# First five pairs of the up projection: low parts of the weight operands and one sum made by accumulating DMAs instead of VectorE

## The chip, the cores and the metric

The kernel runs on one core of a Trainium2 chip. The metric is the device time of one execution in microseconds (us). The kernel before takes 2647.08 us (median of 3 runs, 2645.2 to 2648.05). The core has a matrix engine (TensorE, in the profile PE, with its weight loads as PEld), VectorE (DVE), ScalarE (ACT), GpSimd (POOL) and SyncE (SP). Each takes its instructions in order from its own queue. Transfers (DMAs) are issued by SP, ACT and POOL and run on 16 shared DMA engines.

## The reference

Two layers of an encoder trunk over 1040 positions (16 learned meta tokens and 1024 inputs) with width 1024. Each layer is an attention part followed by a gated feed-forward part. Only the second matters here:

```
def conv_ffn(x, w_up, conv_w, conv_b, w_down):
    h = x @ w_up
    L = h.shape[1]
    hp = jnp.pad(h, ((0, 0), (CONV_W - 1, 0), (0, 0)))
    hc = conv_b
    for j in range(CONV_W):
        hc = hc + hp[:, j:j + L] * conv_w[j]
    u, g = jnp.split(hc, 2, axis=-1)
    return (jax.nn.silu(g) * u) @ w_down

...
        h = h + jnp.concatenate([o_gla, o_fox], axis=-1) @ w_out[i]
        h = h + conv_ffn(rms_norm(h, ffn_norm[i]), w_up[i], conv_w[i], conv_b[i], w_down[i])
```

`w_up` has 2 x 2816 columns: 22 blocks of 128 columns for u and 22 for g. All data is float32.

## The kernel before

**The product scheme.** Every float32 matrix product is made from two parts of each operand: `hi`, the operand rounded to the reduced format that the matrix engine multiplies (fp32r), and `lo`, the operand minus `hi`. Three matmuls (hi x hi, lo x hi, hi x lo; `mm3`, L216 to L218) replace one.

The up projection of a layer (`ffn_up`) takes the 22 pairs (u block j, g block j) one after the other. For each pair the weights form a 2 x 2 block matrix: rows are u and g, columns are the two halves of the 1024 inputs. A11 and A12 are the halves of u, A21 and A22 those of g. The positions are also cut in two halves of 520 (516 in the second layer). A scheme with seven block products instead of eight, numbered p = 1 to 7, is used. Its weight operands are A11 (p = 1), A12 (2), A12 - S2 (3), A22 (4), S1 = A21 + A22 (5), S2 = S1 - A11 (6) and A11 - A21 (7). The other operands, X1 to X7, are made once per layer from the normalised positions. Each product (j, p) is 4 x 2 x 3 = 24 matmuls of 128 x 260 (258) columns.

**The order of products** is written out by hand in `seq`; PE follows it exactly. For the first three pairs it is (0,1) (0,2) (1,1) (1,2) (2,1) (2,2), then (0,6) (1,6) (0,7) (1,7) (0,4) (1,4) (0,5) (1,5) (0,3) (1,3), then the rest of pair 2. From j = 3 on it is (j,2) (j,6) (j,5) (j,7) (j+1,1) (j,4) (j,3). The instructions of the other engines are ordered by a scheduler when the kernel is built, so each engine's queue is fixed before it runs.

**Weight operands.** `ensure(i)` calls `up_operand` for products up to four ahead (`AHEAD = 4`). At the first use of a pair, SP loads the four raw blocks of 128 x 512 (256 KB each). A11 and A12 go to tag `raw` (4 buffers), A21 and A22 to tag `raw2`, whose pool has 7 buffers. `combine` makes S1 and S2 (two more `raw2` buffers) and rewrites A21 and A12 in place, all on VectorE (L997). For (2,1) and (2,2) the blocks of pair 2 are loaded once more, early, each into a `raw2` buffer (L983). `up_split` then makes `hi` with a copy on ACT (L1013) and `lo` with a subtraction on VectorE (L1014). `hi` and `lo` have 3 buffers for even and 3 for odd products. A buffer is reused when the last instruction that reads it has ended.

**X operands.** X1 and X2 are made during the output projection that precedes (`wout`). `second_half` (before product 1) scales the norm of the second half. `make_t23` (before product 2) makes X6 and X7: L1132, L1133 and the splits of `put` (ACT L1037, VectorE L1038). `make_n4` and `make_t1` make X4 and X5 with subtractions on POOL (L1144, L1152), `make_b22` X3. `wout` also stores each block of h to memory from POOL (L1096) and adds squares on POOL (L1102).

**Results.** A product fills a pair of PSUM banks. `place` gives the bank: products p = 2 of the pairs 0, 1 and 2 all use the bank pair `p2`. `evacuate` copies p = 1, 4, 6, 7 out on ACT (L1181) and adds p = 2, 3 and the g sum on VectorE (L1180). So (1,2) waits for VectorE's addition after (0,2), and (2,2) for the one after (1,2). When a pair is complete, `conv` (ACT L1169, VectorE L1173) and the gate follow, and POOL stores the block (`actd`, L1203).

Of the kernel before, what the change touches and what calls it, by code (L numbers as in the profile page):

```python
# [10 lines left out]
F32 = mybir.dt.float32  # L11
# [3 lines left out]
ALU = mybir.AluOpType  # L15
# [33 lines left out]
HALVES, HALVES_LAST = (0, 520, 520), (8, 524, 516)  # L49
AHEAD = 4  # L50
NSPLIT = 4


class Slots:
# [78 lines left out]
class Kern:  # L133
# [731 lines left out]
    def attention(self, lyr, nm, hsrc, chunks, feed):  # L865
        tc, nc, s = self.tc, self.nc, self.slots
        with tc.tile_pool(name=f"aps{lyr}", bufs=2, space=PSUM, reuse_waits="tile") as pp2, \
# [50 lines left out]
            with tc.tile_pool(name=f"att{lyr}", bufs=2, reuse_waits="tile") as ap, \  # L918
# [5 lines left out]
                def plan(p):  # L924
# [11 lines left out]
                    elif p == 4:  # L936
# [10 lines left out]
                        def split(j):  # L947
                            c0, n = CH[j]
                            for k in KORD:
                                self.split(mix[k][0][:, c0:c0 + n], mix[k][1][:, c0:c0 + n], land[k][:, c0:c0 + n])  # L950
                            for m in range(NSPLIT):
                                nc.gpsimd.dma_start(hT[m][:, c0:c0 + n], hsrc[m][:, c0:c0 + n])
                        split(2)
                        for m in range(NSPLIT):
                            def ev(ps, c0, n, m=m):
                                h = hT[m][:, c0:c0 + n]
                                nc.vector.tensor_tensor(out=h, in0=ps, in1=h, op=ALU.add)
# [3 lines left out]
                self.fox(lyr, ap, pp, qs, plan, lambda: box["mix"][KD - 1])  # L961
            for m in range(NSPLIT, KD):
                nc.sync.dma_start(box["hT"][m][:, chunks[0][0]:T], hsrc[m][:, chunks[0][0]:T])
# [15 lines left out]
    def up_operand(self, lyr, j, p, fw, raws, odd):  # L979
        nc = self.nc  # L980
        if j == 2 and p in (1, 2):
            src = fw.tile([128, 4, 128], F32, tag="raw2", name="raw2")
            nc.sync.dma_start(src[:], self.wm[lyr, M_UP + 4][:, 4 * p - 4:4 * p, :])  # L983
            return self.up_split(src, fw, odd)
        if j not in raws:
            u, g = self.wm[lyr, M_UP + 2 * j], self.wm[lyr, M_UP + 2 * j + 1]
            q = raws[j] = {}
            for name, src, k0, own in (("A11", u, 0, True), ("A21", g, 0, False), ("A22", g, 4, False), ("A12", u, 4, True)):
                q[name] = self.wp.tile([128, 4, 128], F32, tag="raw", name="raw", bufs=4) if own else \
                    fw.tile([128, 4, 128], F32, tag="raw2", name="raw2")  # L990
                nc.sync.dma_start(q[name][:], src[:, k0:k0 + 4, :])
        q = raws[j]

        def combine(out, a, b, op):
            if out not in q:
                q[out] = fw.tile([128, 4, 128], F32, tag="raw2", name="raw2")
            nc.vector.tensor_tensor(out=q[out][:], in0=q[a][:], in1=q[b][:], op=op)  # L997
        if p == 6:
            combine("S1", "A21", "A22", ALU.add)
            combine("S2", "S1", "A11", ALU.subtract)  # L1000
        elif p == 7:
            combine("A21", "A11", "A21", ALU.subtract)
        elif p == 3:
            combine("A12", "A12", "S2", ALU.subtract)
        src = q[{1: "A11", 2: "A12", 3: "A12", 4: "A22", 5: "S1", 6: "S2", 7: "A21"}[p]]
        return self.up_split(src, fw, odd)

    def up_split(self, src, fw, odd):
        nc = self.nc
        pool, x = (fw, "2") if odd else (self.wp, "")  # L1010
        hi = pool.tile([128, 4, 128], F32R, tag="hi" + x, name="hi", bufs=3)
        lo = pool.tile([128, 4, 128], F32R, tag="lo" + x, name="lo", bufs=3)
        nc.scalar.copy(hi[:], src[:])  # L1013
        nc.vector.tensor_tensor(out=lo[:], in0=src[:], in1=hi[:].bitcast(F32), op=ALU.subtract)  # L1014
        return [(hi[:, k, :], lo[:, k, :]) for k in range(4)]

    def ffn_up(self, lyr, mix, hT, pp, fw, halves, o0, during_last):
# [65 lines left out]
        def wout(i, h):  # L1083
            m = orders[h][i]
            k0 = KD - 1 if m < NSPLIT else 0

            def f(w):
# [15 lines left out]
                if h == 0:  # L1103
                    return
                if m < NSPLIT:
                    nc.scalar.mul(half(gt, m % 2), x, gain(m))
# [327 lines left out]
```

## Time and profile before

| | |
|---|---|
| median of 3 runs | 2647.08 us (2645.2 to 2648.05) |
| the profiled execution | 2645.09 us |
| its span, first to last instruction | 2643.3 us |
| busy: PE, PEld | 2523.9, 2407.2 us |
| busy: DVE, ACT, POOL | 1759.9, 1240.1, 457.9 us |
| mean granted clock of TensorE | 0.987 |
| matmuls named `up` by line | 3 x 2464 = 7392 |

Times in the profile are microseconds from the start of the span. A row of the timeline gives start, duration, engine, line, operation, output tile <- input tiles, shape, and in brackets how long the engine sat idle before it and what ended that. In the first layer the up projection starts at 612.4 us; its steady part takes about 20.1 us for a pair. Busy time is an average over stages; what an edit is worth is read from the stage that it touches.

### The profile page before, as it was taken

To read this page: it belongs to the slowest core of one execution; us is meant where nothing else is said; L and a number is where in the kernel's file an instruction comes from. 1 tells how busy PE (TensorE), PEld (TensorE's weight loads), DVE (VectorE), ACT (ScalarE), POOL (GpSimd) and SP (SyncE) were. 2 spreads that over 40 slices of the span, in tenths; PEclk is the share of its full clock that TensorE was granted. 3 is DMA by queue.
4 is the path that set the end of the run, shared out by engine and by line. 5 is a ranking of instruction groups with operands and counts; after the bars stand their busy time and mean duration, and the time that the engine had idled before them with its cause. 6 is when DMAs were issued, how large, how long until landed. Compare 5 with 4: busy or idle time off the path is not lost.

```text
span 2643.3 us, 46336 instructions
## 1 busy us (share of the span) xinstructions
PE 2523.9 (95%) x18102; PEld 2407.2 (91%) x18102; DVE 1759.9 (67%) x3484; ACT 1240.1 (47%) x2677; POOL 457.9 (17%) x596
## 2 busy tenths in 40 slices
PE   8999999897999999999999999998989999999997
PEld 7988898897999999999999888887889999998886
DVE  7655676759877777643665666666698767776335
ACT  6345665645544445421343565665455444453112
POOL 4033333333000000000201333332320000000002
PEclk9999999998999999999999999999999999999999
DMA  3222124341222222632312222142512222245222
GB/s 125 65 83 70 47 83 124 106 131 58 97 81 76 85 77 92 217 94 58 103 56 65 75 72 74 56 138 91 158 51 85 83 81 77 83 139 189 65 55 77
DMA packets 114476, 240.72 MB, mean 91 GB/s; under 512 B 14432, under 2 KB 36192, under 8 KB 114256
## 3 DMA queue, kind: packets, MB, share of 16 engines
q1 hardware_dynamic: 96000, 182.27, 22.7%
q0 software_dynamic: 16384, 53.18, 5.5%
q8 instruction: 142, 2.33, 0.4%
q10 hardware_dynamic: 1872, 2.31, 0.2%
q14 instruction: 78, 0.64, 0.1%
HBM read 174.01 MB, written 50.91 MB: 85 GB/s over the span
## 4 chain that ended last, share of the span: by engine, by line
PE 77%; DVE 13%; ACT 4%; issue 3%; DMA 2%; POOL 2%; DVEq 0%; SPq 0%; POOLq 0%; ACTq 0%
PE mm L216 12%; PE mm L217 12%; PE mm L218 12%; PE up L216 10%; PE up L217 10%; PE up L218 10%; PE av L706 2%; PE tr L688 2%; DVE S L655 1%; DVE x L1038 1%; PE wo L217 1%; PE wo L216 1%; PE wo L218 1%; DVE PT L331 1%; ACT P L667 1%
## 5 line engine op out<-in xcount | busy, mean ns | idle before, releaser
L216 PE MATMUL up<-x,hi 128*128 128x260 f32 (+1 forms) x2464 | 701.3, 285 | 22.7 <-DVE hu L1180 20.3
L217 PE MATMUL up<-x,lo 128*128 128x260 f32 (+1 forms) x2464 | 699.2, 284 | 0.0
L218 PE MATMUL up<-x,hi 128*128 128x260 f32 (+1 forms) x2464 | 698.5, 283 | 0.0
L216 PEld LDWEIGHTS up<-x,hi 128*128 128x128 f32 x2464 | 467.5, 190 | 24.4 <-DVE hu L1180 20.7
L217 PEld LDWEIGHTS up<-x,lo 128*128 128x128 f32 x2464 | 467.9, 190 | 0.1
L218 PEld LDWEIGHTS up<-x,hi 128*128 128x128 f32 x2464 | 467.8, 190 | 0.0
L216 PE MATMUL mm<-xh,hi 128*128 128x348 f32 (+4 forms) x1056 | 365.1, 346 | 0.0
L218 PE MATMUL mm<-xl,hi 128*128 128x348 f32 (+4 forms) x1056 | 340.9, 323 | 0.0
L217 PE MATMUL mm<-xh,lo 128*128 128x348 f32 (+4 forms) x1056 | 340.8, 323 | 0.0
L1014 DVE TENSOR_TENSOR lo<-raw,hi 128x512 fp32r<-128x512 f32 x308 | 212.9, 694 | 146.2 <-ACT hi L1013 146.2
L183 ACT CAST hi<-raw 128x512 fp32r<-128x512 f32 (+1 forms) x264 | 142.3, 543 | 329.8 <-PE mm L218 240.0
L217 PE MATMUL mm<-ah,lo 128*128 128x400 f32 (+1 forms) x760 | 266.4, 351 | 0.2 <-DVE lo L185 0.2
L218 PE MATMUL mm<-al,hi 128*128 128x400 f32 (+1 forms) x760 | 265.9, 350 | 0.0
L216 PE MATMUL mm<-ah,hi 128*128 128x400 f32 (+1 forms) x760 | 265.8, 350 | 0.0
L185 DVE TENSOR_TENSOR lo<-raw,hi 128x512 fp32r<-128x512 f32 (+1 forms) x196 | 120.7, 620 | 181.1 <-ACT hi L183 177.5
L1013 ACT CAST hi<-raw 128x512 fp32r<-128x512 f32 x308 | 190.3, 620 | 107.6 <-PE up L218 92.7
L216 PEld LDWEIGHTS mm<-xh,hi 128*128 128x128 f32 x1056 | 201.0, 190 | 6.0 <-issue 5.3
L217 PEld LDWEIGHTS mm<-xh,lo 128*128 128x128 f32 x1056 | 200.9, 190 | 0.4 <-issue 0.3
L218 PEld LDWEIGHTS mm<-xl,hi 128*128 128x128 f32 x1056 | 199.9, 189 | 0.4 <-issue 0.3
L1203 POOL DMA_DIRECT2D actd<-cv x44 | 23.4, 533 | 830.0 <-DVE cv L1202 830.0
L667 ACT ACTIVATE P<-S,m 116x460 f32<-116x460 f32 (+2 forms) x224 | 124.8, 561 | 76.9 <-DVE m L655 72.6
L331 DVE TENSOR_TENSOR PT<-tr,PT 116x464 fp32r<-116x464 f32 (+3 forms) x240 | 122.1, 516 | 55.8 <-ACT PT L330 54.1
(248 smaller groups left out, 5269.0 us busy)
## 6 DMA issues: line engine op xcount, KB each, us to landing
raw<-in_wm_dram SPq DMA_DIRECT2D x328, 256.0 KB, 2.6
raw<-in_wd_dram SPq DMA_DIRECT2D x64, 256.0 KB, 2.6
actd<-cv POOLq DMA_DIRECT2D x22, 520.0 KB, 2.9
st<-actd SPq DMA_DIRECT2D x22, 520.0 KB, 4.9
actd<-cv POOLq DMA_DIRECT2D x22, 512.0 KB, 3.0
st<-actd SPq DMA_DIRECT2D x22, 512.0 KB, 4.8
cb<-cd SPq DMA_DIRECT2D x16, 520.0 KB, 4.2
kA<-kA SPq DMA_DIRECT2D x24, 260.0 KB, 3.8
```

Of the source, the lines that this page charges most:

```text
L183: nc.scalar.copy(hi[:, :n, :], raw[:, :n, :])
L185: eng.tensor_tensor(out=lo[:, :n, :], in0=raw[:, :n, :], in1=hi[:, :n, :].bitcast(F32), op=ALU.subtract)
L216: nc.tensor.matmul(ps, wh, xh[:, c0:c0 + n], start=first, stop=False, skip_group_check=more)
L217: nc.tensor.matmul(ps, wl, xh[:, c0:c0 + n], start=False, stop=False, skip_group_check=more)
L218: nc.tensor.matmul(ps, wh, xl[:, c0:c0 + n], start=False, stop=last, skip_group_check=more)
L331: nc.vector.tensor_tensor(out=lo, in0=src, in1=hi.bitcast(F32), op=ALU.subtract)
L655: nc.vector.tensor_tensor_reduce(out=S[:rows, :n], in0=S[:rows, :n], in1=cb[:rows, c0:k1], scale=1.0, scalar=(BIG if ci == 0 else m[:rows, ...
L667: nc.scalar.activation(P[:rows, :n], S[:rows, :n], AF.Exp, scale=-1.0, bias=m[:rows, nch - 1:nch], accum_out=(den if nch == 1 else d3[:row ...
L688: nc.tensor.transpose(tr[:w, j, :rows], P[:rows, o:o + w], id_)
L706: nc.tensor.matmul(av[:, a:width], w.rearrange("p a b -> p (a b)"), x, start=(t == 0 and i == 0), stop=(t == last and i == 1))
L1013: nc.scalar.copy(hi[:], src[:])
L1014: nc.vector.tensor_tensor(out=lo[:], in0=src[:], in1=hi[:].bitcast(F32), op=ALU.subtract)
```

## The change

For pairs j = 0 to 4 (`N_DMA_LO = 5`) of both layers:

- `lo` is no longer a subtraction on VectorE. ACT writes -hi into the `lo` tile, and a DMA issued by POOL adds the raw block to it in place (`accum_op=ALU.add`).
- S1 is no longer an addition on VectorE. SP loads the first half of g into a `raw2` buffer once more, and a DMA issued by POOL adds the second half to it from memory. This buffer is taken at the first use of the pair, not at p = 6.

The early blocks of (2,1) and (2,2) are treated the same way. S2, A11 - A21 and A12 - S2 stay on VectorE. All other pairs are as before.

```
+N_DMA_LO = 5
...
         if j == 2 and p in (1, 2):
             src = fw.tile([128, 4, 128], F32, tag="raw2", name="raw2")
             nc.sync.dma_start(src[:], self.wm[lyr, M_UP + 4][:, 4 * p - 4:4 * p, :])
-            return self.up_split(src, fw, odd)
+            return self.up_split(src, fw, odd, True)
...
                 nc.sync.dma_start(q[name][:], src[:, k0:k0 + 4, :])
+            if j < N_DMA_LO:
+                q["S1"] = fw.tile([128, 4, 128], F32, tag="raw2", name="raw2")
+                nc.sync.dma_start(q["S1"][:], g[:, 0:4, :])
+                nc.gpsimd.dma_start(q["S1"][:], g[:, 4:8, :], accum_op=ALU.add)
...
         if p == 6:
-            combine("S1", "A21", "A22", ALU.add)
+            if "S1" not in q:
+                combine("S1", "A21", "A22", ALU.add)
             combine("S2", "S1", "A11", ALU.subtract)
...
-        return self.up_split(src, fw, odd)
+        return self.up_split(src, fw, odd, j < N_DMA_LO)
...
-    def up_split(self, src, fw, odd):
+    def up_split(self, src, fw, odd, by_dma):
...
         nc.scalar.copy(hi[:], src[:])
-        nc.vector.tensor_tensor(out=lo[:], in0=src[:], in1=hi[:].bitcast(F32), op=ALU.subtract)
+        if by_dma:
+            nc.scalar.mul(lo[:], hi[:].bitcast(F32), -1.0)
+            nc.gpsimd.dma_start(lo[:].bitcast(F32), src[:], accum_op=ALU.add)
+        else:
+            nc.vector.tensor_tensor(out=lo[:], in0=src[:], in1=hi[:].bitcast(F32), op=ALU.subtract)
```

Counted in the built programs, the queues change by -80 instructions on VectorE, +70 on ACT, +80 DMAs on POOL and +10 loads on SP, over both layers. PE's order is the same, and outside the first pairs so are the other queues.

## The prediction

> **What bounds the kernel now.** I read the page first, then PE's waits, then the timelines around the one wait that matters, then a table of stretches.
>
> ```profile
> span 2643.3 us, 46336 instructions
> PE 2523.9 (95%) x18102; PEld 2407.2 (91%) x18102; DVE 1759.9 (67%) x3484; ACT 1240.1 (47%) x2677; POOL 457.9 (17%) x596
> PE up L216 <- DVE hu L1180: 20.3, 2, 10.2
> PE up L216 <- ACT hu L1181: 2.1, 2, 1.1
> core 0: us, PE busy (x) PEld busy (x) DVE busy (x) ACT busy (x) POOL busy (x), PEclk, DMA share, GB/s
> 628.30:638.40 10.10, 0.00 (x0) 0.00 (x0) 8.98 (x12) 6.09 (x11) 4.36 (x3) 0.61 0.00 1
> 638.40:654.00 15.60, 14.50 (x97) 14.29 (x98) 14.77 (x20) 6.03 (x11) 5.13 (x3) 0.82 0.17 51
> 700.00:720.10 20.10, 20.10 (x170) 20.10 (x169) 14.79 (x20) 9.71 (x14) 0.53 (x1) 1.00 0.22 80
> ```
>
> PE is busy 95% of the span, and in the steady part of the up projection (last row, about one pair) all of the time, with VectorE at 14.79 of 20.10 us. VectorE work saved there buys nothing. The only large PE wait in the up projection is 20.3 us in two pieces, one per layer, for a VectorE addition into `hu`. That is where this change can pay.
>
> ```profile
> 619.65 0.70 DVE L273 SCALAR_TENSOR_TENSOR nt<-nt 128x520 f32<-128x520 f32 x1
> 620.27 0.70 DVE L1180 TENSOR_TENSOR hu<-up,hu 128x520 f32<-128x520 f32 x1
> 620.87 0.70 DVE L274 TENSOR_TENSOR nt<-nt 128x520 f32<-128x520 f32 x1
> 621.48 0.69 DVE L1014 TENSOR_TENSOR lo<-raw,hi 128x512 fp32r<-128x512 f32 x1
> 629.42 0.70 DVE L1038 TENSOR_TENSOR x<-h,x 128x520 fp32r<-128x520 f32 x1 [2.38 <-ACT x L1037]
> 637.71 0.69 DVE L1180 TENSOR_TENSOR hu<-up,hu 128x520 f32<-128x520 f32 x1
> 638.46 0.59 PE L216 MATMUL up<-x,hi 128*128 128x260 f32 x1 [10.25 <-DVE hu L1180]
> 653.80 0.40 PE L216 MATMUL up<-x,hi 128*128 128x260 f32 x1 [1.05 <-ACT hu L1181]
> ```
>
> Product (2,2) needs bank `p2`, which (1,2) filled. The addition that empties it starts at 637.71 and ends at 638.40, because it stands in VectorE's queue behind `make_t23` (X6, X7) and the operand work. Queued instructions follow each other every 0.61 us (619.65, 620.27, 620.87, 621.48).
>
> **What goes and what comes.**
>
> ```profile
> L1014 DVE TENSOR_TENSOR lo<-raw,hi 128x512 fp32r<-128x512 f32 x308 | 212.9, 694 | 146.2 <-ACT hi L1013 146.2
> L997 DVE TENSOR_TENSOR raw<-raw,raw 128x512 f32<-128x512 f32 x176 | 116.0, 698 | 0.2
> L1013 ACT CAST hi<-raw 128x512 fp32r<-128x512 f32 x308 | 190.3, 620 | 107.6 <-PE up L218 92.7 <-DVE raw L997 7.7 <-PE wo L218 7.2
> L1096 POOL DMA_DIRECT2D hm<-h x16: 547/549/562, 557.7 to 613.8; - x16
> L991 SPq DMA_DIRECT2D raw<-in_wm_dram x176: 327/328/433, 540.8 to 2321.7; - x176
> ```
>
> VectorE loses 70 subtractions x 0.694 = 48.6 us and 10 additions x 0.698 = 7.0 us. ACT gains 70 scalings; the nearest row is its cast, 0.620, so 43 us. POOL gains 80 DMA issues x 0.55 = 44 us, SP 10 loads x 0.33 = 3 us. In a steady pair ACT goes from 9.71 to about 9.71 + 7 x 0.62 = 14.1 of 20.1 us and POOL from 0.53 to about 5: neither becomes the bound, and PE covers it. If that cover were gone, the dearest would be ACT with 4.3 us per pair.
>
> The unknown is L, the time from the issue of an accumulating DMA to its landing. No accumulating DMA is in the trace. Nearest rows:
>
> ```profile
> raw<-in_wm_dram SPq DMA_DIRECT2D x328, 256.0 KB, 2.6
> actd<-cv POOLq DMA_DIRECT2D x22, 520.0 KB, 2.9
> kA<-kA SPq DMA_DIRECT2D x24, 260.0 KB, 3.8
> hm<-h POOLq DMA_DIRECT2D x16, 260.0 KB, 2.6
> h<-in_hT_dram POOLq DMA_DIRECT2D x4, 200.0 KB, 5.5
> DMA to landing us min/median/max: 2.3/2.6/4.2
> DMA to landing us min/median/max: 2.9/3.8/6.1
> ```
>
> The last two are for `hm` in the first layer and for `kA`. From below L is the fastest `hm`, 2.3; from above the slowest POOL group, 5.5. The accumulate goes SBUF to SBUF like `kA`, at best 2.9; it also reads its destination, so twice the bytes, and `actd` against `hm` prices 260 KB more at 0.3 (in the finer rows 0.4). I take L = 3.3, nearer the low end, because these DMAs are issued singly.
>
> **The new path to the wait.** In the built program two waits are new, and both come from buffers. The seven `raw2` buffers now hold A21, A22 and S1 of pairs 0 and 1 and the block of (2,1). The block of (2,2) must take the buffer of (2,1), and S2 of pair 0 the buffer of (2,2); each waits until the accumulating DMA that reads the old block has landed. S2 stands on VectorE in the middle of `make_t23`, so everything behind it waits too, the `hu` addition included.
>
> ```profile
> 557.75 0.56 POOL L1096 DMA_DIRECT2D hm<-h  x1 [17.98 <-DVE h L1095]
> 609.67 1.66 ACT L1013 CAST hi<-raw 128x512 fp32r<-128x512 f32 x3 [2.40 <-PE wo L218]
> 613.75 0.55 POOL L1096 DMA_DIRECT2D hm<-h  x1 [7.31 <-DVE h L1095]
> L1038 DVE TENSOR_TENSOR x<-dd,x 128x520 fp32r<-128x520 f32 x4 | 4.9, 1233 | 0.0
> L1038 DVE TENSOR_TENSOR x<-h,x 128x520 fp32r<-128x520 f32 x6 | 4.2, 694 | 2.4 <-ACT x L1037 2.4
> ```
>
> Step by step in the first layer:
> - The DMA for `lo` of (2,1) stands behind the last `hm` store on POOL: 613.75 + 0.55 = 614.3. Its ACT work is done: eight instructions at 1.66 / 3 = 0.55 from 609.67 end at 614.1.
> - It lands at 614.3 + L. SP loads the block of (2,2): 2.6. ACT makes `hi` and -hi: 2 x 0.6. POOL issues, and it lands another L later. S2 starts at 614.3 + 3.8 + 2L = 618.1 + 2L, which is 624.7. VectorE's own queue would get there at 620.27 + 6 x 0.61 = 623.9, so it waits 0.8 us.
> - From S2 to the end of the `hu` addition stand 15 instructions: 15 x 0.61 = 9.2. In the window 612 to 640 the four `x<-dd` took 1.233 instead of 0.694, beside POOL's subtractions; I keep those 4 x 0.54 = 2.2. The addition ends at 624.7 + 11.4 = 636.1 instead of 638.4.
>
> Gain: 2.3 us per layer; the second layer has the same queues and waits and is counted alike. It falls by 2 us for each us of L and is at most 3.1. S2 of pair 1, in the same queue, waits for a second DMA, the `lo` of (0,7). It is issued about 3 us after S2 of pair 0 starts and lands at +6.6; VectorE gets there at +9.7. This wait is hidden up to L of about 6.
>
> The 1.05 us wait (653.80) is for an ACT copy queued behind casts of X5. With the queues 2 us earlier against the products I count it gone: 2.1 us for both layers. If it stays, that is lost.
>
> TensorE's granted clock is 0.61 in the stall and 0.82 in the stretch after it. A full clock there would save 0.18 x 14.5 = 2.6 us per layer. A stall of about 7.8 us is left, so I count nothing and keep 2.6 for the range.
>
> Behind that, pairs 2 to 4 run with every block held until a DMA lands. The tightest place is S2 of pairs 2 and 3: a chain of loads and accumulates (five transfers in a row) stands on VectorE ahead of the g addition that (0,3) needs. By the same prices it is ready 2 to 3 us before PE asks; each us of L takes 2 us of it. The `lo` of the later products land 4 us or more ahead. The `actd` stores, now among the DMAs on POOL, make later `lo` wait for the gate of pairs 0 and 1; that is in the 4 us.
>
> The S1 accumulates of pairs 0 and 1 stand on POOL ahead of the first `hm` store, where it idles 17.98 us, and cost nothing; their loads on SP add 2 x 0.33 us to a queue that runs ahead there.
>
> The sum: 2 x 2.3 + 2.1 = 6.7 us. The profiled execution took 2645.1 (its span and 1.8 around it), so 2638.4. The median of the runs stands 2.0 above that execution: 2640.4, written as 2640.
>
> **A rule against the change.** POOL and VectorE do get in each other's way here:
>
> ```profile
> L1144 POOL TENSOR_TENSOR h<-h,h 128x520 f32<-128x520 f32 (+1 forms) x8 | 14.7, 1843 | 28.7 <-DVE h L1133 28.7
> 559.58 1.31 POOL L1102 TENSOR_TENSOR r<-r,sq 128x520 f32<-128x520 f32 x1
> ```
>
> POOL's subtraction takes 1.843 where the same size took 1.31. But the 16 `hm` issues took 547 to 562 ns in a stretch in which VectorE was mostly busy, and landed in 2.3 to 4.2. The Trainium skill, SBUF — State Buffer, section "SBUF: two separate sides", says that a DMA issued from GpSimd needs GpSimd to write descriptors, and that certain VectorE operations lock it out meanwhile; its example goes from 620 to 3100 ns. The issue rows speak against that here. By its example L would be about 2.5 us longer, 5.8, and the time that of the slower rival.
>
> **The rivals.**
> - *The DMAs land just late enough.* L from 3.7 to 5.2 gives per layer a gain from about 2.5 down to a loss of about 1.5 at the stall, so 2642 to 2650. For it: `kA` at 3.8. Chance 0.24.
> - *Slower: the landing of the accumulate sets the pace.* One mechanism, the chain through the buffers, decided by L. At L = 5.5 S2 starts at 629.1 and the addition ends at 640.5, 2.1 us later than before. The chain ahead of the g addition then is about 2 us late for (0,3), and the 1.05 us is saved: 2 x (2.1 + 2.0 - 1.05) = 6.1 us, 2653. It passes 0.2% at L of about 5.4. For it: POOL's 5.5 us row, the blocking above, and that an add inside a transfer is priced by no row. Chance 0.30.
> - *The stall goes altogether.* 20.3 + 2.1 + 2 x 2.6 = 27.6 us, 2620. Against it: 15 instructions stand between S2 and the addition, and (2,2) could start at 628.3. Chance 0.03, within the faster cases.
>
> **How the numbers follow.** About 0.2% (5.3 us) is what a measurement of this kernel can tell from no change. The forecast, L up to about 3.7, is faster and has 0.43; with the last rival 0.46. Same 0.24, slower 0.30. The low end: 3.1 + 1.05 + 2.6 per layer, 13.5 us, gives 2633.6; with VectorE and POOL no longer colliding, about 2631. The high end is the slower rival at its bound, 2654. The range of the faster cases alone is 2631 to 2642.
>
> **What would show it.** Right: the PE wait for `hu` shrinks to about 7.8 us per layer, (2,2) starts near 636, and VectorE shows a short wait at S2 that ends with a DMA. Accumulating DMAs land in about 3.3. Wrong: landings over 5, VectorE idle before S2 for several us, PE waits for `lo` or for the `hg` addition in pairs 0 to 4, or a PE wait under 4 us.

## The result, and the profile after

The changed kernel is slower. Its median was 2666.34 us against 2646.14 us of the kernel before on the same chip, a ratio of 1.0073 with a 95% interval of 1.0053 to 1.0092. Measured a second time (run `e1_after_again`, the same kernel) it was 2660.18 against 2648.13 us, ratio 1.0045 (1.003 to 1.006). So it loses 12 to 20 us where 7 were forecast as a gain.

The first profile was taken at a granted clock of 0.56, so all rows of the changed kernel below are from the second measurement, at 0.983. The page:

```profile
span 2665.8 us, 46572 instructions
PE 2534.8 (95%) x18102; PEld 2418.2 (91%) x18102; DVE 1712.7 (64%) x3404; ACT 1278.5 (48%) x2747; POOL 526.4 (20%) x676
```

VectorE is 47 us less busy than before; PE is busy 11 us longer, and the span is 22.5 us longer. PE's waits in the up projection (engine and line that waited, what released it, us in total, times, longest):

```profile
PE up L217 <- DVE hg L1192: 10.4, 2, 5.3
PE up L217 <- ACT hi L1021: 10.1, 1, 10.1
PE up L217 <- DVE hu L1192: 7.7, 1, 7.7
PE up L217 <- ACT hu L1193: 3.2, 1, 3.2
```

The 20.3 us for `hu` are now 17.8 (10.1 + 7.7; in the row of 10.1 the `hu` addition ended at 641.66, an ACT cast at the same moment, and the row names the cast). The first line is new: 10.4 us for the `hg` addition. Where each wait stands, from PE's timeline:

```profile
641.80 0.56 PE L217 MATMUL up<-x,hi 128*128 128x260 f32 x1 [10.10 <-ACT hi L1021]
675.58 0.59 PE L217 MATMUL up<-x,hi 128*128 128x260 f32 x1 [5.08 <-DVE hg L1192]
1956.87 0.55 PE L217 MATMUL up<-x,hi 128*128 128x258 f32 x1 [7.73 <-DVE hu L1192]
1971.83 0.58 PE L217 MATMUL up<-x,hi 128*128 128x258 f32 x1 [3.20 <-ACT hu L1193]
1996.16 0.58 PE L217 MATMUL up<-x,hi 128*128 128x258 f32 x1 [5.28 <-DVE hg L1192]
```

641.80 and 1956.87 are (2,2), 1971.83 is (0,7), 675.58 and 1996.16 are (0,3). PE runs the same products in the same order in every kernel here, so the cleanest comparison is the start of each product, counted from the start of (0,1) of its layer, minus the same for the kernel before (us, worked out from PE's timeline; + is late):

| first layer / second layer | (2,2) | (0,7) | (1,7) | (0,3) | (2,6) | (6,6) | end of stage |
|---|---|---|---|---|---|---|---|
| changed kernel | 0.0 / -2.3 | 0.0 / +1.7 | -1.2 / +2.1 | +3.8 / +7.3 | +6.1 / +8.3 | +6.1 / +8.7 | +6.7 / +8.7 |

The two up stages lose 15.4 us. This execution took 2667.6 us, 22.5 more than the profiled one of before; the other 7 arose outside them (3.4 ahead of the first), where executions of one kernel differ too (those of before here: 2643.7 to 2653.2). Of the 15.4, 13.4 appear between (1,7) and (2,6): the wait of (0,3), and the slow clock behind it. In the table of windows (busy time of PE, PEld, DVE, ACT, POOL, then clock, DMA share, GB/s):

```profile
675.60:684.00 8.40, 8.40 (x48) 8.40 (x48) 6.50 (x7) 7.53 (x8) 0.86 (x1) 0.64 0.50 138
```

After the wait PE got a clock of 0.64 for 8.4 us; over the same products of the kernel before it was 1.00. (0,3) took 5.4 us instead of 3.3 in the first layer.

**Why the `hg` addition was late.** POOL's, SP's and VectorE's timelines of the changed kernel ahead of 675.58:

```profile
656.62 1.22 POOL L1024 DMA_DIRECT2D lo<-raw  x1
662.06 0.39 SPq L995 DMA_DIRECT2D raw<-in_wm_dram  x1
669.01 0.89 POOL L996 DMA_DIRECT2D raw<-in_wm_dram  x1 [7.05 <-issue]
669.54 3.03 POOL L1024 DMA_DIRECT2D lo<-raw  x3
674.22 0.69 DVE L1002 TENSOR_TENSOR raw<-raw,raw 128x512 f32<-128x512 f32 x1 [8.58 <-DMA lo<-raw]
674.83 0.69 DVE L1192 TENSOR_TENSOR hg<-up,hg 128x520 f32<-128x520 f32 x1
```

This is one chain. The `lo` of (1,5) is issued at 656.62; only when it has landed may SP load S1 of pair 3 into that buffer (662.06); POOL adds the second half to it (669.01); behind that on POOL stands `lo` of (2,6) (669.54), whose landing frees the buffer for S2 of pair 3. While S2 (674.22) waited for that, VectorE sat idle for 8.58 us, with the `hg` addition queued behind it. VectorE was not short of time but blocked. The landings of these transfers, in order of time: `lo` of (1,5) and (0,3), the load of S1, `lo` of (2,6), (2,5) and (2,7):

```profile
DMA to landing us min/median/max: 5.1/5.1/5.2
DMA to landing us min/median/max: 5.3/5.3/5.3
DMA to landing us min/median/max: 4.6/5.3/6.1
```

The same stretch in the table of windows, after and then before, with the DMA share as the last but one number:

```profile
660.00:675.60 15.60, 10.52 (x89) 10.31 (x87) 3.38 (x5) 5.56 (x11) 4.42 (x5) 0.97 0.86 190
```

```profile
660.00:676.00 16.00, 15.85 (x131) 15.51 (x130) 15.19 (x22) 8.75 (x12) 0.00 (x0) 1.00 0.37 116
```

With the forecast's prices the chain ends at about 666.4 (656.62 + 3.3 + 2.6 + 0.55 for POOL's issue + 3.3), and PE asks at 670.5. It ended at 674.2, 7.8 us later: 1.9 on the first landing, 0.3 until SP issued, 2.7 on the load, 1.6 until POOL issued, 1.3 on the last landing. POOL stood idle for those 1.6 us; most accumulates of S1 here are issued 0.5 to 0.6 us after their load lands, and what held this one longer is not shown. The DMA engines were 86% busy there instead of 37%.

### The profile page after: what moved, and what is told of

Read it like the earlier page. It is cut to its first block, busy times and chain, and to the rows that moved or that the text cites. A ratio compares the mean times of both kernels' runs of the same rounds, so it can differ in the third digit from the quotient of the medians.

```text
span 4051.6 us, 46572 instructions
## 1 busy us (share of the span) xinstructions
PE 4020.3 (99%) x18102; PEld 3486.1 (86%) x18102; DVE 1743.0 (43%) x3404; ACT 1298.7 (32%) x2747; POOL 517.5 (13%) x676
## 4 chain that ended last, share of the span: by engine, by line
PE 98%; DVE 1%; ACT 0%; POOL 0%; DMA 0%; issue 0%; SPq 0%; DVEq 0%; POOLq 0%; ACTq 0%
PE mm L217 15%; PE mm L218 15%; PE mm L219 15%; PE up L219 12%; PE up L217 12%; PE up L218 12%; PE av L707 3%; PE tr L689 3%; PE S L654 2%; PE S L653 2%; PE wo L217 1%; PE wo L219 1%; PE wo L218 1%; PE fo L720 1%; DVE x L1050 0%; PE u L501 0%
## 5 line engine op out<-in xcount | busy, mean ns | idle before, releaser
L217 PE MATMUL up<-x,hi 128*128 128x260 f32 (+1 forms) x2464 | 949.8, 385 | 8.1 <-DVE hu L1192 8.1
L219 PE MATMUL up<-x,hi 128*128 128x260 f32 (+1 forms) x2464 | 949.4, 385 | 0.0
L218 PE MATMUL up<-x,lo 128*128 128x260 f32 (+1 forms) x2464 | 946.9, 384 | 0.0
L217 PEld LDWEIGHTS up<-x,hi 128*128 128x128 f32 x2464 | 670.7, 272 | 9.0 <-ACT x L1049 8.6
L218 PEld LDWEIGHTS up<-x,lo 128*128 128x128 f32 x2464 | 670.5, 272 | 0.4 <-issue 0.2
L219 PEld LDWEIGHTS up<-x,hi 128*128 128x128 f32 x2464 | 668.3, 271 | 0.1
L217 PE MATMUL mm<-xh,hi 128*128 128x348 f32 (+4 forms) x1056 | 504.2, 477 | 0.0
L219 PE MATMUL mm<-xl,hi 128*128 128x348 f32 (+4 forms) x1056 | 476.3, 451 | 0.0
L218 PE MATMUL mm<-xh,lo 128*128 128x348 f32 (+4 forms) x1056 | 475.6, 450 | 0.0
L218 PEld LDWEIGHTS mm<-ah,lo 128*128 128x128 f32 x760 | 169.1, 223 | 74.1 <-issue 29.3
L217 PEld LDWEIGHTS mm<-ah,hi 128*128 128x128 f32 x760 | 167.5, 220 | 74.2 <-issue 31.4
L219 PEld LDWEIGHTS mm<-al,hi 128*128 128x128 f32 x760 | 167.0, 220 | 70.9 <-issue 28.8
```

Of the source, the lines that this page charges most:

```text
L217: nc.tensor.matmul(ps, wh, xh[:, c0:c0 + n], start=first, stop=False, skip_group_check=more)
L218: nc.tensor.matmul(ps, wl, xh[:, c0:c0 + n], start=False, stop=False, skip_group_check=more)
L219: nc.tensor.matmul(ps, wh, xl[:, c0:c0 + n], start=False, stop=last, skip_group_check=more)
```

## The experiments

Summary; the column "up stages" is the sum of both layers at the end of the stage, counted as in the table above, from each run's profile:

| run | median us | before beside it | ratio, 95% interval | up stages us |
|---|---|---|---|---|
| e1 changed kernel | 2660.18 | 2648.13 | 1.0045 (1.003 to 1.006) | +15.4 |
| e2 early blocks on VectorE | 2654.68 | 2648.13 | 1.0027 (1.0014 to 1.0039) | +9.5 |
| e3 two operands back | 2651.29 | 2644.51 | 1.0029 (1.0017 to 1.0041) | +4.8 |
| e4 two pairs | 2647.21 | 2644.51 | 1.0008 (0.9997 to 1.0019) | +0.9 |
| e5 S1 on VectorE | 2652.12 | 2644.51 | 1.0023 (1.0014 to 1.0033) | +3.5 |
| e6 pairs 3 to 7 | 2665.39 | 2644.51 | 1.0073 (1.0053 to 1.0093) | +17.3 |
| e7 S2 behind hg | 2655.05 | 2646.04 | 1.0027 (1.0017 to 1.0037) | +6.5 |
| e8 pairs 3 to 7, S2 behind hg | 2646.05 | 2646.04 | 1.0 (0.999 to 1.0011) | -1.2 |
| e9 two pairs, copy first | 2644.49 | 2646.04 | 0.9988 (0.9978 to 0.9998) | -4.0 |
| e10 five pairs, both orders | 2654.22 | 2646.04 | 1.0028 (1.0017 to 1.0039) | +9.1 |
| e11 S1 on VectorE, copy first | 2646.69 | 2648.27 | 0.9998 (0.9987 to 1.0009) | +1.7 |
| e12 X7 later, no DMA | 2636.72 | 2648.27 | 0.9955 (0.994 to 0.9971) | -9.3 |
| e13 two pairs, X7 later | 2637.79 | 2648.27 | 0.9959 (0.9944 to 0.9974) | -9.6 |
| e14 S1 on VectorE, X7 later | 2639.81 | 2648.27 | 0.9971 (0.996 to 0.9982) | -6.1 |

The last column comes from one execution each and can lie several us from the difference of the medians: in e5 it is 3.5 against 7.6, and the profiled execution (2646.58) is the fastest of its ten.

**The changed kernel again.** No edit.

> The changed kernel again, unaltered, for a profile at full clock; about 2666 us, 10 us per layer more than before. Three theories of where these stand. (A) The chain through the buffers: the landing of the accumulating DMA is longer than 3.3 us at full clock (5 or more), S2 of pair 0 waits on VectorE for it, and the wait of TensorE for the hu addition before (2,2) is longer than the 10.2 us of before, some 15 to 20. (B) The wait before (2,2) is 7 to 9 us as forecast, and TensorE waits instead for lo, for the hg addition or for S2's descendants in pairs 0 to 4, 12 us or more per layer in several pieces. (C) The queues of ACT and POOL: the 35 scalings and 40 issues per layer push the X operands (X6, X7, X4, X5) back, and TensorE waits for x, not for hu or lo.

Theory B of that text (waits in pairs 0 to 4) holds with the 5 us at (0,3), not with 12 in several pieces; A fails, as the stall did not grow.

**The early blocks on VectorE.**

```
-            return self.up_split(src, fw, odd, True)
+            return self.up_split(src, fw, odd, False)
```

> As the changed kernel, but lo of the two early blocks (2,1) and (2,2) is made by VectorE as before. Their buffers then come free without a DMA in the chain of two landings. (A) The chain through the buffers: most of the loss goes, the time is 2640 to 2650 us and TensorE's wait before (2,2) is about 10 us or less. (B) or (C): the loss stays within 4 us of the changed kernel's, 2660 to 2668 us.

Between the two: 2654.68. The stall before (2,2) did not shrink (10.2 and 10.0 us), but that does not clear the chain. Without its wait, VectorE reaches the work behind S2 while POOL makes X4, and four of its instructions per layer take about 1.8 us instead of 0.69, 4.4 us in all (two such in the kernel before, 2.2 us):

```profile
627.06 1.81 DVE L1050 TENSOR_TENSOR x<-h,x 128x520 fp32r<-128x520 f32 x1
```

The wait of (0,3) fell to 3.2 us in both layers, though this edit is some 45 us away from it. How it reaches there was not followed.

**Two operands back.** Of 40 accumulating DMAs per layer, the two that head the chain above go back to VectorE.

```
-            if j < N_DMA_LO:
+            if j < N_DMA_LO and j != 3:
                 q["S1"] = ...
-        return self.up_split(src, fw, odd, j < N_DMA_LO)
+        return self.up_split(src, fw, odd, j < N_DMA_LO and (j, p) != (2, 6))
```

> As the changed kernel, but S1 of pair 3 and lo of (2,6) are made by VectorE again: 2 of the 40 accumulating DMAs per layer are gone. These two stand ahead of S2 of pair 3 on VectorE, and that ahead of the hg addition that (0,3) waits for. Theory H (head of the queue): the 5 us wait before (0,3) and the slow clock behind it, together about 7 us per layer, go away; the time is 2643 to 2650 us. Theory T (traffic): the landings are long because the DMA engines are nearly full around there, 38 of 40 transfers remain, so the wait stays within 2 us of its size and the time is above 2655 us.

The wait of (0,3) went from 5.1 and 5.3 us to none and 0.3, and the delay at (2,6) from +6.1 / +8.3 to -0.2 / +1.8. The time, 2651.3, is 1 us above H's range and 4 below T's: what is left is waits for copies by ACT (6.5 us), of which below, and for `lo` (2.3 us).

**Two pairs.**

```
-N_DMA_LO = 5
+N_DMA_LO = 2
```

> As the changed kernel, but only pairs 0 and 1 and the early blocks of pair 2 go by DMA (16 lo and 2 S1 per layer instead of 35 and 5). Both H and T: the wait before (0,3) goes away, as S2 of pairs 2 and 3 need no DMA of pairs 2 and 3. What it tells: the front part alone, the wait before (2,2). By the forecast's own sum (2.3 + 1.05 us per layer at the stall) 2641 us; if the first layer's stall stays at 10 us as in the changed kernel, about 2645 us.

2647.2, within 0.2% of before. The gain at the stall came (-2.4 / -1.3 at (2,2)) and was given back: PE waited 1.0 and 1.2 us for `lo` of (1,6), and then at (0,7). PE's and ACT's timelines of this run:

```profile
647.39 0.39 PE L217 MATMUL up<-x,hi 128*128 128x260 f32 x1 [1.87 <-ACT hu L1193]
645.70 1.15 ACT L1049 CAST x<-h 128x520 fp32r<-128x520 f32 x2 [1.09 <-DVE h L1163]
646.76 0.58 ACT L1193 COPY hu<-up 128x520 f32<-128x520 f32 x1
```

(0,7) needs the bank of (0,6), which ACT empties with the `hu` copy; the copy stands behind casts of X operands that wait for VectorE and POOL. PE came there 3 us earlier than before, ACT did not.

**S1 on VectorE.**

```
-            if j < N_DMA_LO:
+            if j < 0:
                 q["S1"] = ...
```

> As the changed kernel, but S1 of all five pairs is an addition on VectorE again; lo stays on DMAs. S2 of pair 3 still waits for lo of (2,6). H: lo of (2,6) no longer queues on POOL behind the accumulate of S1 of pair 3, which waits for its own load, so it lands 5 us earlier and most of the wait before (0,3) goes; 2645 to 2652 us. T: 2655 us or more.

2652.1, at the edge of H. No wait at (0,3) and none later, with all 70 `lo` still on DMAs; the loss left in the profiled execution is the copy wait of (0,7), 5.1 us in the first layer, and in the second a stall of 11.6 us. One kernel, two patterns: in the first layer POOL's first subtraction for X4 took 8.99 us, no VectorE instruction in the stall was long, and the stall was 6.9; in the second POOL's took 1.7 and four of VectorE's about 1.8 instead of 0.69.

**Pairs 3 to 7.**

```
-            if j < N_DMA_LO:
+            if 3 <= j < N_DMA_LO + 3:
...
-        return self.up_split(src, fw, odd, j < N_DMA_LO)
+        return self.up_split(src, fw, odd, 3 <= j < N_DMA_LO + 3)
```

The early blocks are made by VectorE.

> The same edit in the steady part: lo and S1 by DMA for pairs 3 to 7, pairs 0 to 2 as before. No X operands, no bank shared between pairs. If the operation itself costs TensorE nothing once PE covers it: 2647 us, same as before. If the DMA engines' load of some 90 percent delays lo in every pair, TensorE waits for lo several times and the time is 2652 us or more.

2665.4: no cheaper than in the first pairs. But PE did not wait for `lo`:

```profile
PE up L217 <- DVE hg L1192: 11.5, 8, 2.9
```

Four waits per layer, before (0,3), (3,3), (4,3) and (5,3), each for the `hg` addition; with the slow clock 17 us. It is the same place in each pair.

**S2 behind the hg additions.** All 80 DMAs stay; one VectorE instruction per layer moves (an order of issue only, no wait).

```
-                add(q["g"][:, t1], q["x"])
+                self.hg_add[j] = add(q["g"][:, t1], q["x"])
...
+            if j == 3:
+                with self.tc.issue_after(self.hg_add[1].ins):
+                    combine("S2", "S1", "A11", ALU.subtract)
```

> The changed kernel with all of its 80 accumulating DMAs; only one instruction per layer stands elsewhere in VectorE's queue: S2 of pair 3 behind the two hg additions of pairs 0 and 1 instead of ahead of them. Theory H (the wait is one of queue order): the 5 us wait before (0,3) and the 2 us of slow clock behind it go in both layers, about 12 us in all, and the time is 2646 to 2652 us. Theory T (the DMA engines are too full): S2 was only the place where it showed; TensorE waits for lo or hu soon after and the time stays above 2656 us.

2655.1, between the theories. The wait of (0,3) is gone in both layers (-2.0 in the first layer at (0,3), where it was +3.8). But 2.7 us came back at (2,7) in the first layer and 3.2 at (0,7) in the second. H is right on the wait and wrong on the sum.

**Pairs 3 to 7 with S2 behind the hg addition.** As e6, with S2 of pair j behind the `hg` addition of pair j - 1 (pair 3: of pair 1).

> Pairs 3 to 7 by DMA, as in the run of these pairs before (its waits for the hg addition before (0,3), (3,3), (4,3), (5,3): 7 us in the first layer, 4 in the second, some 17 us in all with the slow clock), but S2 of each of these pairs stands behind the hg addition of the pair ahead of it. H: all of these waits go and the time is 2645 to 2650 us, that of the kernel before: the operation itself is then free where TensorE covers it. T: 2655 us or more.

2646.05 against 2646.04: the 17 us are gone, by order alone. Three steady pairs in the table of windows:

```profile
700.00:760.00 60.00, 60.00 (x504) 60.00 (x503) 29.92 (x33) 41.16 (x63) 22.26 (x27) 1.00 0.89 197
```

and its DMA issues there, with the median landing:

```profile
lo<-raw POOLq DMA_DIRECT2D x21, 256.0 KB, 4.6
raw<-in_wm_dram SPq DMA_DIRECT2D x15, 256.0 KB, 5.2
```

PE is busy for all 60 us with the DMA engines at 0.89, landings of 4.6 and loads of 5.2. In this order full DMA engines cost PE nothing, so T falls; and saving 14 us of VectorE (44.03 us busy in these 60 before) brings nothing either.

**Two pairs, copy first.** As e4, and ACT's casts of X5 stand behind the copies of (0,6) and (1,6).

```
-                copy(q["u"][:, t1])
+                self.hu_copy = copy(q["u"][:, t1])
...
-                put(5, k, y)
+                with self.tc.issue_after(self.hu_copy.ins):
+                    put(5, k, y)
```

> Pairs 0 and 1 and the early blocks of pair 2 by DMA, and on ACT the casts of X5 stand behind the copies of (0,6) and (1,6) out of their banks. In the run without this order the stall before (2,2) was 1.6 to 2.7 us shorter and 1.9 to 3.2 us of it came back as a wait of (0,7) for the copy of (0,6). If the copy is late only because it queues behind casts that wait for POOL, that wait goes: 2 to 3.5 us per layer, 2638 to 2642 us. If the copy's own place is not it (ACT is simply full by its extra scalings), no gain: 2645 to 2648 us.

2644.5, 2 us short of what was expected: the copy wait fell from 1.9 and 3.2 to 1.1 and 1.2 us, and a wait for `lo` of 1.0 at (1,6) stayed. The copy order without any DMA was not run, so it is open how much of the 4.0 us it gives alone; the copy wait of the kernel before is 1.05 us per layer.

**Five pairs, both orders.** e7 and e9 together, all 80 DMAs.

> All 80 accumulating DMAs, S2 of pair 3 behind the hg additions, and the X5 casts behind the copies of (0,6) and (1,6). H: both waits that the change brought are gone and what the forecast counted on is left, the shorter stall before (2,2): 2638 to 2645 us. T: above 2652 us.

2654.2, the number of T, though T itself fell with e8. Up to (1,5) it stood at -1.9 / -1.3, then waits for `lo` at (1,3) and for a copy at (2,7). PE's, VectorE's and ACT's timelines of this run:

```profile
682.96 0.39 PE L218 MATMUL up<-x,hi 128*128 128x260 f32 x1 [3.16 <-ACT hu L1200]
678.84 0.69 DVE L1003 TENSOR_TENSOR raw<-raw,raw 128x512 f32<-128x512 f32 x1 [3.85 <-DMA raw<-in_wm_dram]
680.84 1.07 ACT L1217 ACTIVATE cv<-cv 128x1040 f32<-128x1040 f32 x1 [4.73 <-DVE cv L1192]
682.33 0.57 ACT L1200 COPY hu<-up 128x520 f32<-128x520 f32 x1
```

VectorE waits for a late raw block, ACT for VectorE's convolution behind that, the copy stands behind ACT's activation, and PE waits for the copy. SP issued that load at 674.06, just as an accumulate landed (674.00). By the built program the block's buffer is that of S1 of pair 2, which the DMA for `lo` of (2,5) reads; no row names the buffer. Mending one queue passed the wait on to the next.

**S1 on VectorE, copy first.** e5 with the order of e9.

> lo of five pairs by DMA, S1 on VectorE, and the X5 casts on ACT behind the copies of (0,6) and (1,6). Theory B (the second loaded buffer for S1, taken at the first use of a pair, is what makes the waits at (0,3) and (2,7), since seven buffers then hold up SP's next loads): neither wait appears, the copy wait of (0,7) shrinks to about 1 us, and the time is 2641 to 2648 us. Theory T (70 accumulating DMAs are too many for these queues whatever the buffers): waits at (0,3) or in pair 2 stay and the time is 2652 us or more.

2646.7, as B says, with no wait at (0,3) or (2,7). The copy wait of (0,7) was a miss: none in the second layer, still 4.4 us in the first. POOL's and ACT's timelines of the first layer:

```profile
627.99 10.25 POOL L1156 TENSOR_TENSOR h<-h,h 128x520 f32<-128x520 f32 x2 [5.68 <-DVE h L1145]
641.30 0.63 ACT L1049 CAST x<-h 128x520 fp32r<-128x520 f32 x1 [2.41 <-POOL h L1156]
650.71 0.58 ACT L1194 COPY hu<-up 128x520 f32<-128x520 f32 x1
```

The first of POOL's two subtractions for X4 took 8.99 us, as in e5. ACT's casts of X4 waited for POOL, VectorE's splits for them, ACT's later casts for VectorE, and the copy stood behind those. In the second layer POOL's subtractions took 1.7 us each; the copy was in time, but the stall before (2,2) was 11.8 us.

**X7 later, no DMA.** The kernel before, with the order of e9 and the four X7 splits behind the `hu` addition.

```
-            operand(7)
+        def make_x7():
+            operand(7)
             for k in range(4):
-                put(7, k, diff(k))
+                with self.tc.issue_after(self.hu_add.ins):
+                    put(7, k, diff(k))
...
-        before = {1: second_half, 2: make_t23, 7: make_n4, ...}
+        before = {1: second_half, 2: make_t23, 4: make_x7, 7: make_n4, ...}
```

> The kernel before, without any accumulating DMA, but with two orders changed: the four splits of X7 on VectorE stand behind the hu addition of (1,2), and the X5 casts on ACT behind the copies of (0,6) and (1,6). If the 10 us stall before (2,2) is one of queue order, as its row says, it shrinks by the four splits, 2.4 to 4.9 us per layer, and the 1 us of (1,7) goes: 2634 to 2641 us. If VectorE's total work there decides, (0,6) or (0,7) waits for X6 or lo in turn: 2643 to 2648 us.

2636.7 us, faster than both kernels. PE's and VectorE's timelines:

```profile
629.56 0.69 DVE L1184 TENSOR_TENSOR hu<-up,hu 128x520 f32<-128x520 f32 x1
630.31 0.58 PE L216 MATMUL up<-x,hi 128*128 128x260 f32 x1 [3.81 <-DVE hu L1184]
652.51 0.41 PE L216 MATMUL up<-x,hi 128*128 128x260 f32 x1 [2.31 <-ACT hg L1185]
```

The stall of 10.25 is 3.81 us. Some 4 us come back at (1,4), 2.3 as a wait for a copy again and the rest as slow clock.

**Two pairs, X7 later.** Both orders, with the DMAs of e4.

> Pairs 0 and 1 and the early blocks by DMA, with both orders of the run before it. The two gains add if DMA takes work from VectorE that then bounds this stretch: 2 to 3 us per layer below the same orders without DMA, 2630 to 2637 us. If order was all, the time is that of the run without DMA, or above it by new waits for lo: 2636 to 2644 us.

```profile
PE up L218 <- DMA lo<-raw: 6.1, 2, 3.9
```

2637.8, the same as without DMAs: (2,2) starts no earlier in sum (-6.6 / -5.6 against -6.4 / -6.4), and (1,6) waits for a landing.

**S1 on VectorE, X7 later.** e11 with the X7 order.

> lo of five pairs by DMA, S1 on VectorE, both orders. By theory B no wait beyond pair 1, so like two pairs with both orders, 2630 to 2640 us. By theory T waits in pairs 2 to 4 of 3 us or more per layer, above 2640 us.

2639.8, just within B's range; with PE 4 to 5 us earlier the `hg` wait before (0,3) is back at 1.3 and 2.1 us.

## Why the prediction was wrong

**What bounds the kernel** was read rightly: a shorter stall before (2,2) pays (e12 starts (2,2) 6.4 us earlier per layer and keeps 4.9 and 4.4 of it, about 1 of them from the copy of (1,7)), and the steady part gives nothing for VectorE time (e8).

**The path to the wait** was right in kind, and its size came out right by luck. S2 of pair 0 waited for a DMA, as said, and in the first layer the two landings ahead of it took 3.9 and 3.3 us:

```profile
629.41 1.11 DVE L1002 TENSOR_TENSOR raw<-raw,raw 128x512 f32<-128x512 f32 x1 [1.86 <-DMA lo<-raw]
634.11 3.28 DVE L1050 TENSOR_TENSOR x<-dd,x 128x520 fp32r<-128x520 f32 x1
633.67 3.15 POOL L1156 TENSOR_TENSOR h<-h,h 128x520 f32<-128x520 f32 x2
```

The forecast was a gain of 2.3 us per layer. It was 2.3 in the second layer (a wait of 7.73, forecast about 7.8), but there two errors cancel: S2 started 14.2 us after (0,1), forecast 12.1, and from S2 to the end of the `hu` addition it was 9.2 us, forecast 11.4, because the 2.2 us kept for VectorE beside POOL did not come. In the first layer of this execution there was no gain: S2 started at 13.5, and 12.25 us followed, with one `x<-dd` of 3.28 us beside POOL. With the same front part e10 gained 2.4 and 2.0, e7 1.3 and 1.5.

**"The 1.05 us wait ... I count it gone"** failed in the second layer (in the first it is gone). It is the copy that empties a bank for the next product; when PE comes earlier and ACT does not, it is late for (0,7) instead: 3.20 us here, 1.9 and 3.2 in e4. The gain at the stall and this wait cancel: e4 shows -0.0 / +0.9 us in the end.

**"By the same prices it is ready 2 to 3 us before PE asks"** is the step that made the sign wrong. By the working above, those prices do give 2 us of lead or more; measured, the addition was 5.1 and 5.3 us late, and 1 to 2 us of slow clock came with it. The mis-sized term is L, and with it the load of 2.6: L was taken from transfers issued singly and used as a constant. Near 657 to 670 it was 5.1 and 4.6 us on this chain, the load 5.3. The change itself fills the DMA engines that the chain waits for (0.86 against 0.37), and landings go with that: over the traces of e1 to e14, the `lo` accumulates issued where the DMA share within 4 us was under 0.4 landed in 3.3 us in the median (50 of them), as forecast, and those above 0.9 in 5.2 (196). Each link was also counted without a delay to issue, but POOL issued 1.6 us after the load had landed. Over the whole run, the median landings:

```profile
lo<-raw POOLq DMA_DIRECT2D x70, 256.0 KB, 4.3
raw<-in_wm_dram POOLq DMA_DIRECT2D x10, 256.0 KB, 4.6
```

and the groups by line:

```profile
L1024 POOL DMA_DIRECT2D lo<-raw x70 | 62.2, 975 | 111.2 <-ACT lo L1023 88.1 <-PE up L219 7.0 <-PE up L218 6.7
L1023 ACT ACTIVATE lo<-hi 128x512 fp32r<-128x512 f32 x70 | 43.2, 628 | 1.3
```

The other prices held (ACT 0.628 for 0.62), but POOL's issue took 0.975 on average, not 0.55.

**The slower rival** was right in mechanism and place: a chain of loads and accumulates through the buffers, late for (0,3), from L of about 5.4. Its price of 2 us per layer there was too small (5.1 and 5.3 measured), and its longer stall, 2.1 us per layer, did not come. It raised L to 5.5 but left the load at 2.6, where 5.3 was measured.

**"The `lo` of the later products land 4 us or more ahead"** failed too, at a small price: PE waited 0.5 us for `lo` of (1,6) in the second layer here, 1.0 and 1.2 in e4, and up to 1.9 for that of (1,3) in e10.

**The lockout.** The Trainium skill, SBUF — State Buffer, section "SBUF: two separate sides", has a DMA issued from GpSimd starve for its descriptors while VectorE runs certain operations. The late landings here do not show it: VectorE was busy for 3.38 of the 15.6 us in which they took 4.6 to 6.1, and SP's load in the same stretch was late as well (5.3).

**Cause, as far as shown.** The wait of (0,3) is one of queue order: S2 of pair 3 ahead of the `hg` additions (e3, e7; e6 and e8 for other pairs). The second is S1's own path, with the buffer that it takes early: without it neither (0,3) nor (2,7) waits, with 70 DMAs left (e5, e11). That fits the held buffers of the chain, but these runs also have 10 accumulates and 10 loads fewer, and an extra `raw2` buffer was not run, so the number of buffers by itself stays open. That the landings are long because the DMA engines are full rests on the counts above; no run changed that alone.

## What to carry to other kernels

When work moves from an engine to a DMA, draw the whole in-order queue behind each new wait, on every engine, and price each landing at the DMA load that the change itself brings, not at that of a lone transfer. An instruction that waits for a DMA belongs behind those that PE waits for: order alone turned 17 us of loss into none (e8), and order without any DMA took 9.3 us off the two up stages (e12). The moved work added next to nothing to that for two pairs (9.6 in e13) and took from it for five (6.1 in e14). When a stall shrinks, look at once for the next thing that the same engines owe PE.

## What the runs showed of the hardware

An accumulating DMA of 256 KB takes about twice the DMA engine time of a plain load of 256 KB. The queues in the same 60 us (700 to 760) of the kernel before and of e8, packets, MB and share of 16 engines:

```profile
q1 hardware_dynamic: 1725, 3.14, 16.2%
q0 software_dynamic: 432, 1.60, 6.5%
```

```profile
q0 software_dynamic: 3851, 7.81, 68.0%
q1 hardware_dynamic: 2160, 3.93, 20.3%
```

12 loads take 16.2% of 960 engine-us, 13.0 each, and the 15 loads of e8 also 13.0 each; 24 accumulates take 61.5 points more than the stores of before, 24.6 each. The Trainium skill, Collectives: The Full Stack, section "The bandwidth ceiling: the fold count and why AG ≠ RS ≠ AR", says that ReduceScatter, which adds inside its transfers, runs at half of AllGather's rate because the add reads two sources; the ratio of 1.9 here, outside any collective, agrees.

Who pays when VectorE and POOL work on tiles at the same time changes from run to run, and even between the layers of one kernel: in the changed kernel one `x<-dd` took 3.28 us beside two POOL subtractions in 3.15; in e4 the same instruction took 0.68 and POOL's two took 7.64.

```profile
628.51 0.68 DVE L1050 TENSOR_TENSOR x<-dd,x 128x520 fp32r<-128x520 f32 x1
628.08 7.64 POOL L1156 TENSOR_TENSOR h<-h,h 128x520 f32<-128x520 f32 x2
```

The stall before (2,2) goes with this. In the profiles of before and of e1 to e11 there are 24 up stages. In 13 of them one of POOL's subtractions for X4 took 5 us or more, VectorE's long instructions ahead of (2,2) (over 0.9 us instead of 0.69) cost 0 to 1.9 us in all, and (2,2) started 23.5 to 24.6 us after (0,1). In the other 11 POOL's took at most 2.9 us, VectorE's cost 2.1 to 4.4, and (2,2) started at 25.8 to 28.1. No run separates this from VectorE's shorter queue. When POOL pays, the X operands behind it come later, and with them ACT's copy for (0,7) (e5, e11).

And the changed kernel spreads more: 2653.2 to 2671.2 us over ten runs, against 2643.7 to 2653.2 of the kernel before beside it.
